# Two DMA queues put in a new order: plain loads and stores on SP, quarter loads alone on the ACT ring, twelve whole pairs transposed by VectorE

## The chip, the cores and the metric

One core of one Trainium2 chip. The metric is device time in microseconds (us) of a whole execution. For one core, the state of a run is told from the other runs of the same kernel on the same chip: a run over 1.5% above the fastest is called slow and is left out of the ratios.

## The reference

```python
y = np.matmul(x, weight)                       # x: (16, 512, 768) f32, weight: (768, 768)
y = y.reshape(16, 512, 12, 64)                 # 12 heads of 64
y1, y2 = y[..., :32], y[..., 32:]
out1 = y1 * cos1 - y2 * sin1                   # rotary embedding: cos, sin of (512, 64),
out2 = y2 * cos2 + y1 * sin2                   # the same for every batch and head
out = np.concatenate([out1, out2], axis=-1).reshape(16, 512, 768)
```

A product of 8192 x 768 by 768 x 768 in half precision, and two multiplications and an addition per element after it.

## The kernel before

The 64 row tiles (128 rows by 768) are worked in 32 *pairs*. For a pair (n; halves s = 0, 1): SP loads the two tiles; ScalarE casts them to fp16 (`xc`); the tile is transposed to `xT`; TensorE does 24 matmuls into PSUM (`psy`); VectorE multiplies by cos and sin at once (`tq`, 3.36 us a pair); GpSimd adds (`ov`, 3.46 us a pair); the pair is stored with one DMA.

There are two ways to get `xT`. The plain way is six TensorE transposes into PSUM and a copy by ScalarE (0.80 us). The other leaves TensorE out: the tile is loaded in four *quarters*, each 32 partitions with rows of 768 bytes, so that VectorE's transpose in blocks of 32 x 32 (0.57 us) gives the whole transposition. Before, ten tiles go this way.

```python
    AHEAD = 7
    AHEAD_B = 6
    ALONE = 4
    def by_blocks(n, s):                       # ten tiles: second halves of pairs 9, 11, ... 27
        return s == 1 and n % 2 == 1 and 8 < n < NP - ALONE
    ...
    xpool = ctx.enter_context(tc.tile_pool(name="xpool", bufs=10))
    bpool = ctx.enter_context(tc.tile_pool(name="bpool", bufs=3))
    ...
    def load_blocks(n):
        ...
        for q in (0, 2, 1, 3):                 # half of the quarters on each queue
            eng = nc.sync if q % 2 == 0 else nc.scalar
            eng.dma_start(out=dst[ts(q, R)], in_=src[r, q])
    ...
    def upto(what, k):                         # casts and transposes run ahead of the matmuls,
        k += min(6, max(0, k - 31) // 4)       # and further ahead as the kernel goes on
        while done[what] < min(k, 2 * NP):
            n, s = divmod(done[what], 2)
            done[what] += 1
            if what == "cast":
                cast(n, s, nc.scalar)
            elif not by_blocks(n, s):
                transpose(n, s, nc.scalar)     # six on TensorE, then ScalarE's copy xT
    ...
    for n in range(2, NP):
        load_plain(n + AHEAD - 2)              # SP
        if n + 1 < NP and by_blocks(n + 1, 1):
            transpose_blocks(n + 1, 1)         # VectorE
        for s in (0, 1):
            for c in CHUNKS:
                mm(n, s, *c)
            upto("turn", 2 * n + s + 3)
            upto("cast", 2 * n + s + 5)
            ...                                # the last four pairs, half by half
        load_blocks(n + AHEAD_B)               # SP and ACT
        if n < NP - ALONE:
            if n >= 3:
                store(n - 3, nc.scalar)        # ACT
            rope_pair(n, ...)                  # VectorE and GpSimd
```

The order of instructions on each engine is that of the program: each engine's work, and the issues of SP and of ScalarE, run so without an exception. A transfer is issued by the engine that it is written on (SP, or ScalarE for the ACT ring), and no work that stands behind an issue of ScalarE began before that issue was over, the soonest 0.04 us after it. So an issue that has to wait holds up all that stands behind it (the trace below has ScalarE stand so until 86.29 us).

## Time and profile before

163.46 us, median of three runs (162.96 to 163.48). The profiled run (163.1 us, granted clock 0.991):

| | before |
|---|---|
| TensorE busy | 150.3 us of a span of 161.3 (93%) |
| one pair in the middle (from one multiply of VectorE to the next) | 4.57 and 4.23 us in turn |
| six transposes on TensorE | 0.33 to 0.35 us |
| half-idle DMA engines | about 121 to 137 us |
| longest stop of ScalarE for a transfer of the other queue whose data it did not need | 2.6 us |

The difference between 4.57 and 4.23 us is one tile's transposes. The lines themselves are in the prediction below.

### The profile page before, as it was taken

To read this page: it belongs to the slowest core of one execution; us is meant where nothing else is said; L and a number is where in the kernel's file an instruction comes from. 1 tells how busy PE (TensorE), PEld (TensorE's weight loads), DVE (VectorE), ACT (ScalarE), POOL (GpSimd) and SP (SyncE) were. 2 spreads that over 40 slices of the span, in tenths; PEclk is the share of its full clock that TensorE was granted. 3 is DMA by queue.
4 is the path that set the end of the run, shared out by engine and by line. 5 is a ranking of instruction groups with operands and counts; after the bars stand their busy time and mean duration, and the time that the engine had idled before them with its cause. 6 is when DMAs were issued, how large, how long until landed. Compare 5 with 4: busy or idle time off the path is not lost.

```text
span 161.3 us, 2793 instructions
## 1 busy us (share of the span) xinstructions
PE 150.3 (93%) x1110; PEld 95.1 (59%) x1110; DVE 120.6 (75%) x70; ACT 91.6 (57%) x115; POOL 110.4 (68%) x41
## 2 busy tenths in 40 slices
PE   7789899999999999999998999999999999999920
PEld 2345566666566666666665666656666666665610
DVE  0555967876668788987878488885878697699980
ACT  3340867666677485656584977488767887200000
POOL 0000297778776787878878757788678776999990
PEclk9999999999999999999999999999999999999996
DMA  4999999999999999999999999999996555399655
GB/s 142 356 406 399 401 403 357 289 344 403 306 403 370 355 387 286 397 353 359 334 318 318 407 328 411 378 349 409 391 406 266 195 195 196 150 393 380 247 200 195
DMA packets 23757, 53.17 MB, mean 330 GB/s; under 512 B 2368, under 2 KB 7872, under 8 KB 23744
## 3 DMA queue, kind: packets, MB, share of 16 engines
q1 hardware_dynamic: 11952, 26.09, 46.5%
q10 hardware_dynamic: 11792, 26.91, 44.1%
q8 instruction: 8, 0.13, 0.3%
q14 instruction: 5, 0.04, 0.1%
HBM read 27.82 MB, written 25.17 MB: 328 GB/s over the span
## 4 chain that ended last, share of the span: by engine, by line
PE 61%; DMA 24%; ACT 5%; SPq 2%; POOL 2%; DVE 1%; issue 1%; ACTq 1%; POOLq 0%; DVEq 0%
PE psy L169 51%; DMA xs<-in_x_dram 17%; PE pt L126 8%; DMA w_raw<-in_weight_dram 4%; DMA xb<-in_x_dram 3%; ACT xc L76 3%; PE psz L169 2%; ACT xT L76 2%; POOL ov L194 2%; DVE tq L183 1%; SPq L83 1%; ACTq L243 1%; SPq L102 1%; POOLq L364 0%; POOLq L194 0%
## 5 line engine op out<-in xcount | busy, mean ns | idle before, releaser
L194 POOL TENSOR_TENSOR ov<-tq 128x1536 f32<-128x1536 f32 (+2 forms) x37 | 110.2, 2988 | 46.8 <-DVE tq L183 46.8
L169 PE MATMUL psy<-w_sb,xT 128*128 128x512 f16 (+1 forms) x732 | 127.5, 326 | 1.0 <-ACT xT L76 0.9
L183 DVE TENSOR_TENSOR tq<-psy,csn 128x3072 f32<-128x3072 f32 (+3 forms) x39 | 103.0, 2658 | 27.9 <-PE psy L169 26.2
L169 PEld LDWEIGHTS <-xT 128*128 128x128 f16 x768 | 73.1, 98 | 45.2 <-ACT xT L76 1.2
L76 ACT COPY xT<-pt 128x768 f16<-128x768 f16 x52 | 41.3, 800 | 38.0 <-PE pt L126 29.1
L76 ACT CAST xc<-xs 128x768 f16<-128x768 f32 x52 | 45.9, 903 | 8.8 <-DMA xs<-in_x_dram 8.7
L126 PEld LDWEIGHTS <-xc 128*128 128x128 f16 x324 | 22.1, 98 | 10.2 <-ACT xc L76 1.9
L126 PE MATMUL pt<-ident,xc 128*128 128x128 f16 x324 | 26.4, 219 | 1.8 <-ACT xT L76 0.7
L76 ACT CAST xc<-xb 128x768 f16<-128x768 f32 x10 | 9.1, 908 | 0.0
L247 PE MATMUL cold_ps<-cold 128*128 128x512 f16 x16 | 5.9, 516 | 1.2 <-DVE cold L252 1.2
L169 PE MATMUL psz<-w_sb,xT 128*128 128x512 f16 (+1 forms) x36 | 6.3, 326 | 0.0
L133 DVE STREAM_TRANSPOSE xT<-xc 128x384 f32<-128x384 f32 x10 | 5.7, 568 | 0.0
L110 DVE CAST w_sb<-w_raw 128x768 f16<-128x768 f32 x6 | 3.4, 560 | 2.1 <-DMA w_raw<-in_weight_dram 2.1
L78 DVE CAST xc<-xs 128x768 f16<-128x768 f32 x2 | 1.9, 946 | 3.6 <-DMA xs<-in_x_dram 3.6
L183 DVE TENSOR_TENSOR tq<-psz,csn 128x512 f32<-128x512 f32 (+1 forms) x5 | 4.3, 897 | 0.1
L247 PEld LDWEIGHTS <-cold 128*128 128x128 f16 x16 | 1.8, 127 | 3.4 <-issue 2.2
L78 DVE COPY xT<-pt 128x768 f16<-128x768 f16 x2 | 1.1, 558 | 1.7 <-PE pt L126 1.7
L76 ACT ACT_TABLE_LOAD x1 | 1.3, 1283 | 1.1 <-PEq L350 1.1
L252 DVE MEMSET cold<- 128x256 uint32 x1 | 0.3, 272 | 0.9 <-PEq L350 0.9
L148 PE MATMUL psy<-cold 128*128 128x512 f16 x2 | 0.8, 379 | 0.0
L226 DVE TENSOR_TENSOR ov<-psz,tq 128x512 f32<-128x512 f32 x1 | 0.7, 691 | 0.0
L222 DVE TENSOR_TENSOR psz<-psz,csn 128x512 f32<-128x512 f32 x1 | 0.7, 690 | 0.0
(8 smaller groups left out, 1.7 us busy)
## 6 DMA issues: line engine op xcount, KB each, us to landing
out_dram<-ov ACTq DMA_DIRECT2D x28, 768.0 KB, 6.5
xs<-in_x_dram SPq DMA_DIRECT2D x54, 384.0 KB, 6.9
out_dram<-ov ACTq DMA_DIRECT2D x7, 384.0 KB, 2.3
w_raw<-in_weight_dram SPq DMA_DIRECT2D x6, 384.0 KB, 7.7
xb<-in_x_dram SPq DMA_DIRECT2D x20, 96.0 KB, 5.6
xb<-in_x_dram ACTq DMA_DIRECT2D x20, 96.0 KB, 4.7
out_dram<-ov SPq DMA_DIRECT2D x1, 256.0 KB, 2.8
csn<-in_cos_dram SPq DMA_DIRECT2D x1, 128.0 KB, 7.8
```

Source lines behind the costliest of these rows:

```text
L76: eng.copy(out=o, in_=i_)
L78: eng.tensor_copy(out=o, in_=i_)
L83: nc.sync.dma_start(out=xss[n, s], in_=x[b].rearrange("(p r) h -> r p h", r=SB)[r])
L102: eng.dma_start(out=dst[ts(q, R)], in_=src[r, q])
L110: nc.vector.tensor_copy(out=w_sb[:, t, e], in_=w_raw[:, t, e])
L126: nc.tensor.transpose(pt[:, t, e, :], xc[:, t, e, :], ident)
L133: nc.vector.transpose(out=xT.bitcast(FP32).rearrange("p t m e -> p (t m e)"), in_=x16.pop((n, s)).bitcast(FP32),)
L169: nc.tensor.matmul(ps, xTT[n, s][:, t, e, :], w_sb[:, t, e, lo:hi], start=((t, e) == CHUNKS[0] and not joined), stop=((t, e) == CHUNKS[-1] ...
L183: nc.vector.tensor_tensor(out=tqs[n][:, :, c0:c1].rearrange("p j (h d) -> p j h d", d=D), in0=ps.rearrange("p (h d) -> p h d", d=D) .unsqu ...
L194: eng.tensor_tensor(out=ovs[n][:, ds(c0, w)].rearrange("p (h t d) -> p h t d", t=2, d=HD), in0=tq[:, 0].rearrange("p (h t d) -> p h t d", ...
L243: eng.dma_start(out=dst, in_=src)
L247: nc.tensor.matmul(cold_ps, cold[:, 0:P], cold, start=True, stop=True)
```

## The change

Twelve whole pairs (7, 9, ... 29) go by VectorE's blocks, so 24 tiles instead of ten. SP carries all plain loads and, except in the tail, all stores, in one program order. ScalarE, which used to issue the stores, now issues only the quarter loads before the tail: two at a time, each holding one quarter of both halves of the pair (192 KB), three and two iterations before the iteration that casts the pair. The intent: fewer transposes on TensorE, no ScalarE standing before a store, and no plain load stuck behind small pieces (in the trace of before, 3 KB packets of SP's queue took up to 2.25 us, 0.12 us in the median).

```diff
-    AHEAD_B = 6
     ALONE = 4
+    BLOCKS = range(7, NP - 2, 2)
 ...
-    xpool = ctx.enter_context(tc.tile_pool(name="xpool", bufs=10))
+    xpool = ctx.enter_context(tc.tile_pool(name="xpool", bufs=8))
 ...
+    def load_quarters(n, quarters):
+        b, r = where(n, 0)
+        if quarters[0] == 0:
+            xss[n] = bpool.tile([P, 2, H], FP32, tag="xb", name="xb")
+            xss[n, 0], xss[n, 1] = xss[n][:, 0], xss[n][:, 1]
+        src = ...
+        for q in quarters:
+            nc.scalar.dma_start(out=dst[ts(q, R)], in_=src[r, q])
 ...
+    def goal(k):
+        return k + min(6, max(0, k - 31) // 4)
 ...
             if what == "cast":
                 cast(n, s, nc.scalar)
-            elif not by_blocks(n, s):
+            elif n in BLOCKS:
+                transpose_blocks(n, s)
+            else:
                 transpose(n, s, nc.scalar)
+    def cast_in(m):                            # the iteration that casts pair m
+        return next(n for n in range(NP) if goal(2 * n + 6) > 2 * m)
 ...
-        load_blocks(n + AHEAD_B)
+        for m in BLOCKS:
+            for lead, quarters in ((3, (0, 2)), (2, (1, 3))):
+                if n == cast_in(m) - lead:
+                    load_quarters(m, quarters)
         if n < NP - ALONE:
-            if n >= 3:
-                store(n - 3, nc.scalar)
+            store(n - 2, nc.sync)
```

More of the change, by code (lines that the diff above doesn't have):

```diff
@@ L41 @@
     AHEAD = 7
-    AHEAD_B = 6
     ALONE = 4
+    BLOCKS = range(7, NP - 2, 2)
     def where(n, s):
         return 2 * (n // SB) + s, n % SB
-    def by_blocks(n, s):
-        return s == 1 and n % 2 == 1 and 8 < n < NP - ALONE
     konst = ctx.enter_context(tc.tile_pool(name="konst", bufs=1))
@@ L85, in load, with load_pair @@
         )
-    def load_plain(n):
+    def load_pair(n):
         for s in (0, 1):
-            if n < NP and not by_blocks(n, s):
+            if n < NP and n not in BLOCKS:
                 load(n, s)
-    def load_blocks(n):
-        if n >= NP or not by_blocks(n, 1):
-            return
-        b, r = where(n, 1)
-        xss[n, 1] = bpool.tile([P, H], FP32, tag="xb", name="xb")
-        src = x[b].rearrange("(j a r) (q k) -> r q a j k", r=SB, a=R, q=NQ)
-        dst = xss[n, 1].rearrange("p (j k) -> p j k", j=NQ)
-        for q in (0, 2, 1, 3):
-            eng = nc.sync if q % 2 == 0 else nc.scalar
-            eng.dma_start(out=dst[ts(q, R)], in_=src[r, q])
+    def load_quarters(n, quarters):
[3 more added lines that the diff above has]
+            xss[n, 0], xss[n, 1] = xss[n][:, 0], xss[n][:, 1]
+        src = x[b : b + 2].rearrange("b (j a r) (q k) -> r q a (b j) k", r=SB, a=R, q=NQ)
+        dst = xss[n].rearrange("p s (j k) -> p (s j) k", j=NQ)
+        for q in quarters:
+            nc.scalar.dma_start(out=dst[ts(q, R)], in_=src[r, q])
     wv = weight.rearrange("(p t e) n -> t e p n", t=NT, e=2)
@@ L115, in cast @@
         src = xss.pop((n, s))
-        if by_blocks(n, s):
+        if n in BLOCKS:
             src = src.rearrange("p (j a t e) -> p t (j a) e", j=NQ, t=NT, e=2)
@@ L254 @@
     for n in (0, 1):
-        load_plain(n)
+        load_pair(n)
     for t, e in CHUNKS:
@@ L260 @@
     for n in range(2, AHEAD):
-        load_plain(n)
+        load_pair(n)
     done = {"cast": 4, "turn": 4}
+    def goal(k):
+        return k + min(6, max(0, k - 31) // 4)
     def upto(what, k):
-        k += min(6, max(0, k - 31) // 4)
+        k = goal(k)
         while done[what] < min(k, 2 * NP):
@@ L311 @@
     for n in range(2, NP):
-        load_plain(n + AHEAD - 2)
-        if n + 1 < NP and by_blocks(n + 1, 1):
-            transpose_blocks(n + 1, 1)
+        load_pair(n + AHEAD - 2)
         for s in (0, 1):
@@ L324 @@
                     store(n, nc.scalar, s * H, (s + 1) * H)
-        load_blocks(n + AHEAD_B)
+        for m in BLOCKS:
+            for lead, quarters in ((3, (0, 2)), (2, (1, 3))):
+                if n == cast_in(m) - lead:
+                    load_quarters(m, quarters)
         if n < NP - ALONE:
-            if n >= 3:
-                store(n - 3, nc.scalar)
+            store(n - 2, nc.sync)
             rope_pair(n, H if n == NP - ALONE - 1 else 2 * H)
         if n == NP - ALONE - 1:
-            for m in (n - 2, n - 1, n):
-                store(m, nc.scalar)
+            for m in (n - 1, n):
+                store(m, nc.sync)
     rope_last(NP - 1, 1)
```

## The prediction

> **What bounds the kernel now.** I read the busy line and the 40 slices first, then the chain that ended last, the waits, and the timeline of the middle, last the windows for the DMA rate.
>
> The page, busy line and slices:
>
> ```profile
> PE 150.3 (93%) x1110; PEld 95.1 (59%) x1110; DVE 120.6 (75%) x70; ACT 91.6 (57%) x115; POOL 110.4 (68%) x41
> ...
> PE   7789899999999999999998999999999999999920
> ...
> DMA  4999999999999999999999999999996555399655
> GB/s 142 356 406 399 401 403 357 289 344 403 306 403 370 355 387 286 397 353 359 334 318 318 407 328 411 378 349 409 391 406 266 195 195 196 150 393 380 247 200 195
> ```
>
> TensorE is full from slice 4 to the tail. The DMA engines are full too, but only to slice 30 (about 121 us): then all of x is loaded, and some 16 us run at half load. So TensorE binds, and DMA is a close second with a reserve at the end.
>
> The waits, whole run (engine, whom it waited for, total, times, longest):
>
> ```profile
> ACT xT L76 <- PE pt L126: 29.1, 37, 1.9
> DVE tq L183 <- PE psy L169: 26.2, 28, 2.1
> ...
> ACT xT L76 <- DMA xb<-in_x_dram: 2.6, 1, 2.6
> ACT xT L76 <- DMA xs<-in_x_dram: 2.2, 1, 2.2
> ...
> PE psy L169 <- ACT xT L76: 0.9, 2, 0.7
> ```
>
> ScalarE and VectorE wait for TensorE, hardly the other way round. The chain of work, in order of time (start, us, what), around one of the rare stalls:
>
> ```profile
> 73.84 1.95 PE psy L169 x12
> 75.79 0.35 PE pt L126 x6
> ...
> 78.58 7.95 DMA xs<-in_x_dram
> 86.53 0.02 issue
> 86.55 0.02 ACTq L243
> 86.56 0.04 issue
> 86.60 0.41 ACTq L243
> 87.01 0.04 issue
> 87.05 0.81 ACT xT L76
> 87.91 2.12 PE psy L169 x12
> ```
>
> Two readings. First, the price list of TensorE: the 12 matmuls of a row tile cost 1.95 us, its six transposes 0.33 to 0.35 us. Second, the stall: ScalarE, which issues the stores, stood before a store until a *load* landed at 86.53, though no data ties them. The trace's records show all transfers rotating over eight completion semaphores in program order, so a transfer waits for the landing of the eighth before it, on whichever queue. That held up ScalarE's copy xT, and TensorE behind it.
>
> Check of the bound: from 16.87 to the last matmul at 154.15 are 137.3 us. 61 tiles x 1.95 = 119.0, plus 50 transposed tiles x 0.335 = 16.8, makes 135.7. So 1.6 us are stalls, all else is TensorE work.
>
> [...] the windows show 401 GB/s at 8 to 24 us, before any quarter load, and much less while quarters fly:
>
> ```profile
> 8.00:24.00 16.00, 15.04 (x111) 9.20 (x111) 11.02 (x12) 8.38 (x11) 4.67 (x2) 1.00 1.03 401
> 28.00:30.00 2.00, 2.00 (x18) 1.35 (x17) 1.43 (x1) 1.30 (x3) 2.00 (x1) 1.00 1.03 263
> 40.90:43.40 2.50, 2.33 (x19) 1.39 (x18) 1.29 (x2) 1.57 (x3) 2.25 (x1) 1.00 1.10 273
> 61.40:62.60 1.20, 1.20 (x14) 0.84 (x12) 1.20 (x1) 0.00 (x0) 1.20 (x1) 1.00 0.72 113
> ```
>
> (last columns: DMA share and GB/s). [...] both queues together never pass 411 GB/s in a slice.
>
> **The change, part by part.**
>
> *TensorE.* Before, ten tiles (second halves of odd pairs 9 to 27) are transposed by VectorE; after, both halves of pairs 7, 9, ... 29, that is 24. Fourteen tiles lose six transposes: 14 x 0.335 = 4.7 us off the engine that binds. The tail (pairs 28 to 31 alone, some 20 us from the end of pair 27's matmuls) keeps its work, so this passes to the end undiminished if nothing else binds.
>
> *ScalarE.* 14 copies xT x 0.80 = 11 us go. Of its issues the 36 stores fall to 8 and the 20 quarters grow to 48, about 0.4 us each: +8 us. It was idle enough; about even. What counts is that it no longer stands before a store: the waits of 2.2 and 2.6 us shown above should go, and with them perhaps 1 us of the 1.6 us of stalls.
>
> *VectorE.* 14 more block transposes at 568 ns: +8.0 us, to 128.6. In the middle a block pair needs 3.36 + 2 x 0.57 = 4.50 us of VectorE against 3.90 us of TensorE; the plain pair after it 3.36 against 3.90 + 0.67 = 4.57. Over two pairs: 7.86 against 8.47 us, 93% full, so it still fits. One joint is tight: early on, when little lead has built up, the first half's transpose comes right after the multiply of the pair before, ending 0.1 + 3.36 + 0.57 = about 4.0 to 4.1 us after that pair's last matmul, and TensorE wants it after 3.90. I estimate 0.2 us for each of pairs 7 to 17: about 1.2 us. (Before, a whole tile time more was left.)
>
> *DMA.* Bytes stay, 53.2 MB: at 403 GB/s, 132 us. Per block tile, 3 KB rows become four 768 B pieces. The 24 slices from 24 to 121 us have a mean of 361 GB/s, so 97 x (1 - 361/403) = 10 us were lost over ten block tiles, about 1 us each. Part of this is the stretch at 61 us (113 GB/s), where the records show plain-load packets stuck up to 2.2 us behind quarters on the same queue; quarters alone on the ACT queue should end that. I put the loss at 0.5 us for each of 24 tiles: 12 us. The sum 132 + 2 (start) + 12 = 146 us, plus 2 to 3 us around 22 us where SP has loaded its seven pairs and must wait for the first store before it goes on, fits into 157 us but uses up most of the reserve. Per two pairs DMA needs 3.15 MB / 403 = 7.8 us plus 2 x 0.5 = 8.8 us against TensorE's 8.47: slightly too slow through the middle, paid from the lead of loads over matmuls, and caught up after pair 29 is loaded.
>
> *One order on SP.* A load of pair n+6 comes after the store of pair n-2, which is ready when GpSimd's add ends, about 0.1 + 3.36 + 0.1 + 3.46 = 7.0 us after that pair's matmuls. The load then has three pairs (some 13 us) until its cast early on, against a median of 6.9 us to landing. The quarters 1 and 3 have only about 6.6 us, and each is twice as large as before (192 KB, where 96 KB took 4.7 to 5.6 us). I estimate another 1 us of stalls in all from late quarters and late loads.
>
> Sum: -4.7 - 1.0 + 1.2 + 1.0 = -3.5; 163.46 - 3.5 = 160.0. The order is evidently matched (two quarters and a store in each pair, two plain loads in every second: eight transfers in two pairs, so each waits for its like of two pairs ago), which makes me lean a little lower: **159.7 us**.
>
> **The rivals.** *DMA becomes the bound.* For it: DMA is full to 121 us, and 24 tiles in small pieces at the old loss of 1 us make 24 us: 132 + 2 + 3 + 24 = 161, no room left; that gives 162 to 166. Against it: the worst stretches belong to SP's mixed queue, and all loads are in at 121 us, eight pairs before they are needed. *VectorE becomes the bound in the middle*, its in-order transposes waiting for casts and delaying the multiply that frees PSUM: 161 to 163. Against it: casts run two tiles ahead, and the waits show VectorE idle 26.2 us for TensorE. *All goes well*: the saved transposes and most old stalls: 163.46 - 4.7 - 1.3 = 157.5.
>
> **Range and chances.** Best case 157.5, a mild DMA shortage 162.5: the range is 157.2 to 162.8. The line for 2% is 160.2, just above my centre, so faster 0.55, within 2% 0.40, slower (over 166.7, only if DMA binds outright) 0.05.
>
> **What would show each step.** Right: transposes x240 instead of x324 in TensorE's group, stream transposes x24 at 568 ns, the two-pair period near 8.5 us (before 8.8) in the middle, TensorE's busy time near 145 us, no wait of ScalarE's copies for a store's semaphore, the half-idle DMA stretch at 125 to 140 us gone or short. Wrong: ScalarE's casts waiting for xb several times by over 1 us and TensorE for xT behind them (quarters late); TensorE waiting for VectorE's xT by more than 0.3 us a pair (the tight joint is worse); slices staying under 350 GB/s with no idle stretch after (DMA binds); or plain loads landing late because SP stands before stores.

The sum stands at -4.7 - 1.0 + 1.2 + 1.0 = -3.5, so 160.0 us, and 159.7 with the lean.

## The result, and the profile after

The changed kernel took 174.16 us, median of four runs (173.54 to 176.84), against 163.47 us of before in the same rounds. The ratio is 1.0657 (95% interval 1.0613 to 1.07): slower by 6.6%. A ratio here is the mean time of one kernel's fast runs over that of the other's in the same rounds, so it is not quite the ratio of the medians.

The profiled run after is the longest of the four (176.84 us, state slow), but the state is not what makes it slow: the three fast runs, of 173.54 to 174.44 us, have mean clocks of 0.953 to 0.962, hardly better than its 0.953. The low clock is part of the effect, as the windows below show. From the page, in this order the busy line, the slices of TensorE and its granted clock, and the two groups of transposes (busy us and mean ns after the first bar, idle time before them after the second):

```profile
PE 151.3 (86%) x1026; PEld 92.1 (53%) x1026; DVE 127.2 (73%) x84; ACT 81.4 (46%) x101; POOL 110.3 (63%) x41
...
PE   7889999999989999996089999899339999999940
...
PEclk9999999999999999999957999999966999999996
...
L124 PE MATMUL pt<-ident,xc 128*128 128x128 f16 x240 | 20.5, 223 | 8.0 <-ACT xc L73 7.3
...
L131 DVE STREAM_TRANSPOSE xT<-xc 128x384 f32<-128x384 f32 x24 | 13.0, 561 | 6.5 <-ACT xc L73 6.4
```

The work is as planned: 240 transposes on TensorE instead of 324, 24 on VectorE. But there are two holes in TensorE's row, in slice 19 and in slices 28 and 29 (counted from 0), and the clock is low just after each. In the middle the kernel otherwise runs better than before. Times of a pair, from the start of VectorE's multiply of the pair before it to that of its own, read from the traces:

| pair | 9 to 15, each | 16 | 19 | 23 | start of pair 26 |
|---|---|---|---|---|---|
| before | 4.23 / 4.57 | 4.57 | 4.57 | 4.23 | 133.92 us |
| after | 4.23 | 13.74 | 6.35 | 12.16 | 147.71 us |

So nearly all the loss lies in three pairs (of the others only pair 8 is much longer than before, 5.42 us against 4.57). Counted over 4.23 us, the three cost 9.51 + 2.12 + 7.93 = 19.6 us; against their own times before, 18.9 us. The kernel is 13.8 us late at pair 26, so the other pairs have *gained* 5.1 us.

The waits after (total, times, longest), and the first of SP's queue:

```profile
ACT xT L73 <- issue: 17.3, 2, 9.7
...
PE psy L167 <- ACT xT L73: 7.5, 3, 6.6
```

```profile
SPq L241 <- POOL ov L192: 93.4, 28, 13.3
```

ScalarE stands idle before its copy xT twice, for 17.3 us together, and TensorE waits for it. "issue" means that nothing which the copy itself needs was missing: ScalarE was busy with, or standing before, something else in its order. SP, meanwhile, spends its time standing before stores until GpSimd's add is done. The timeline around the first hole (start, us, what, and in brackets the idle time before it) shows what ScalarE stood before:

```profile
79.74 4.61 SPq L241 DMA_DIRECT2D out_dram<-ov  x2
...
81.01 0.50 PE L124 MATMUL pt<-ident,xc 128*128 128x128 f16 x6
...
86.29 0.94 ACTq L100 DMA_DIRECT2D xb<-in_x_dram  x2
87.27 0.80 ACT L73 COPY xT<-pt 128x768 f16<-128x768 f16 x1 [9.69 <-issue]
...
88.13 6.79 PE L167 MATMUL psy<-w_sb,xT 128*128 128x512 f16 x24 [6.62 <-ACT xT L73]
```

The transposes of 81.01 were done by 81.5, and their copy could have begun then. It began at 87.27, because ScalarE issued two quarter loads at 86.29 first. Those loads need no data that the kernel computes, and their buffer was free: the first two quarters of the same pair had gone into it at 74.70 and 75.14. The issue and landing times of single transfers in the records, with the semaphore that each raises when it lands, tell why they were late:

```
semaphore 99   store of pair 11 (SP)              issued 71.26   landed 78.51
semaphore 99   store of pair 13 (SP)              issued 79.74   landed 86.27
semaphore 99   first of the late quarter loads    issued 86.29
               of pair 19 (ACT ring)
```

All transfers of the kernel share eight semaphores, numbered 99, 101, 103, 104, 105, 107, 108 and 109. The built program gives them out in turn, in the order in which it lists the transfers. Each transfer waits for the landing of the one that had its semaphore before, on whichever queue that was: of the 134 transfers in this trace 126 have such a forerunner, and all of them went out after it had landed, the soonest 0.02 us after. Here the quarter load, which stands *ahead* of pair 13's store in the source by one iteration, was given that store's semaphore after it. It could not be issued before a store that was itself waiting for GpSimd.

The smaller loss, in pair 19, has the same cause: a quarter load went out at 106.18, 0.02 us after the store of pair 16 (SP) had landed on its semaphore, and ScalarE's copy behind it came after 5.78 us of idle. Here VectorE lost the time: its block transposes, which stand before the multiply of pair 19 in its order, waited 1.00 and 0.92 us for ScalarE's casts. Pairs 20 and 21 then took only 3.72 and 3.85 us.

The second hole is the same as the first, on the chain that ended last (start, us, what):

```profile
117.07 7.66 DMA out_dram<-ov
...
124.75 0.34 ACTq L100
...
129.71 0.82 PE pt L124 x6
130.53 3.84 PE psy L167 x12
```

A store lands at 124.73, and only then does ScalarE's next load (L100 is the quarter load) go out. The last two lines show the after-effect: 12 matmuls took 3.84 us and six transposes 0.82, against 1.95 and 0.35 in the kernel before. The windows after the first hole (columns: window, busy us and counts of PE, PEld, DVE, ACT and POOL, then granted clock, DMA share, GB/s) show why:

```profile
84.00:86.00 2.00, 0.00 (x0) 0.00 (x0) 0.64 (x1) 0.00 (x0) 1.28 (x1) 1.00 0.86 341
86.00:88.00 2.00, 0.00 (x0) 0.00 (x0) 0.00 (x0) 0.73 (x2) 2.00 (x1) 0.71 0.99 249
...
90.00:92.00 2.00, 2.00 (x9) 0.97 (x7) 0.24 (x1) 1.87 (x3) 0.00 (x0) 0.50 1.10 225
92.00:94.00 2.00, 2.00 (x9) 1.05 (x8) 0.00 (x0) 0.00 (x0) 0.00 (x0) 0.58 1.06 383
94.00:96.00 2.00, 2.00 (x18) 1.26 (x16) 0.98 (x1) 0.71 (x2) 0.00 (x0) 1.00 0.31 114
```

The clock fell to half (0.50 from 90 to 92 us) some 5.3 us into the idle time, at 86.8 by the mean of that window, and came back at 93.7 by that of its own, 5.5 us after the work had resumed. So 24 matmuls took 6.79 us where they take 3.90. This closes the sum of pair 16: 6.62 us of waiting and 2.89 us of slow matmuls are 9.51 us, and 13.74 less 4.23 is 9.51.

### The profile page after: what moved, and what is told of

It is laid out like the page before. It is cut to its first block, busy times and chain, and to the rows that moved or that the text cites. A ratio compares the mean times of both kernels' runs of the same rounds, so it can differ in the third digit from the quotient of the medians.

```text
span 175.0 us, 2632 instructions
## 1 busy us (share of the span) xinstructions
PE 151.3 (86%) x1026; PEld 92.1 (53%) x1026; DVE 127.2 (73%) x84; ACT 81.4 (46%) x101; POOL 110.3 (63%) x41
## 4 chain that ended last, share of the span: by engine, by line
POOL 33%; PE 30%; issue 15%; DMA 12%; DVE 3%; ACTq 2%; SPq 1%; ACT 1%; POOLq 1%; DVEq 0%
POOL ov L192 33%; PE psy L167 24%; DMA out_dram<-ov 4%; DMA xs<-in_x_dram 4%; DMA w_raw<-in_weight_dram 4%; PE pt L124 3%; DVE tq L181 3%; ACTq L100 2%; PE psz L167 2%; SPq L80 1%; ACT xc L73 1%; POOLq L371 0%; POOLq L192 0%; DVEq L181 0%; ACT xT L73 0%
## 5 line engine op out<-in xcount | busy, mean ns | idle before, releaser
L167 PE MATMUL psy<-w_sb,xT 128*128 128x512 f16 (+1 forms) x732 | 130.3, 334 | 7.6 <-ACT xT L73 7.5
L167 PEld LDWEIGHTS <-xT 128*128 128x128 f16 x768 | 75.0, 100 | 56.5 <-ACT xT L73 8.2
L73 ACT COPY xT<-pt 128x768 f16<-128x768 f16 x38 | 30.3, 800 | 52.9 <-PE pt L124 28.2
L73 ACT CAST xc<-xs 128x768 f16<-128x768 f32 x38 | 33.2, 904 | 15.4 <-DMA xs<-in_x_dram 10.7
L124 PE MATMUL pt<-ident,xc 128*128 128x128 f16 x240 | 20.5, 223 | 8.0 <-ACT xc L73 7.3
L124 PEld LDWEIGHTS <-xc 128*128 128x128 f16 x240 | 16.7, 100 | 15.7 <-ACT xc L73 9.9
L73 ACT CAST xc<-xb 128x768 f16<-128x768 f32 x24 | 21.4, 902 | 2.6 <-DMA xb<-in_x_dram 2.6
L131 DVE STREAM_TRANSPOSE xT<-xc 128x384 f32<-128x384 f32 x24 | 13.0, 561 | 6.5 <-ACT xc L73 6.4
```

Source lines behind the costliest of these rows:

```text
L73: eng.copy(out=o, in_=i_)
L124: nc.tensor.transpose(pt[:, t, e, :], xc[:, t, e, :], ident)
L131: nc.vector.transpose(out=xT.bitcast(FP32).rearrange("p t m e -> p (t m e)"), in_=x16.pop((n, s)).bitcast(FP32),)
L167: nc.tensor.matmul(ps, xTT[n, s][:, t, e, :], w_sb[:, t, e, lo:hi], start=((t, e) == CHUNKS[0] and not joined), stop=((t, e) == CHUNKS[-1] ...
```

## The experiments

The theory to test: *ScalarE is stopped by shared completion semaphores; the new order of transfers pairs its quarter loads with transfers of SP that stand behind a store.* The rivals: *B*, the DMA engines cannot carry 24 tiles in 768-byte pieces; *C*, VectorE has become the bound; *D*, plain loads come too late because SP stands before stores. All runs were correct. e1 to e4 share one chip and one set of runs of before, e5 to e8 another set, e9 to e11 a third.

| run | median us | ratio to before [95%] | longest pair of 9 to 25, us |
|---|---|---|---|
| after | 174.16 | 1.0657 [1.0613, 1.07] | 13.74 |
| e1 no growing lead | 168.38 | 1.0321 [1.0263, 1.0379] | 4.47 |
| e2 quarters on SP | 163.34 | 1.0015 [0.9955, 1.0075] | 7.47 |
| e3 seven block pairs | 170.93 | 1.0477 [1.0435, 1.0518] | 12.45 |
| e4 eight block pairs | 170.57 | 1.0462 [1.0419, 1.0504] | 12.95 |
| e5 quarters on SP, loads nine pairs ahead | 159.1 | 0.9633 [0.9558, 0.9708] | 5.23 |
| e6 stores on ACT | 160.97 | 0.98 [0.9735, 0.9864] | 5.62 |
| e7 stores on ACT, loads nine ahead | 164.94 | 1.0034 [0.9965, 1.0104] | 5.35 |
| e8 loads nine ahead alone | 178.76 | 1.0882 [1.0802, 1.0962] | 13.33 |
| e9 seven 4-byte loads, spread | 179.43 | 1.089 [1.0798, 1.0982] | 8.22 |
| e10 seven 4-byte loads, early | 173.01 | none (one fast run, 168.9 us) | 4.24 |
| e11 e5 with eleven pairs ahead | 161.18 | 0.9795 [0.97, 0.989] | 7.36 |

### e1: without the growing lead

In the changed kernel two sets of quarter loads fall together where the lead of the casts grows (iterations 13, 16 and 21). Without the growth there is one set in every iteration, and two quarter loads and a store in each pair with two plain loads in every second pair make exactly eight transfers per two pairs.

```diff
     def goal(k):
-        return k + min(6, max(0, k - 31) // 4)
+        return k
```

> The changed kernel with the growing lead of casts and transposes taken out (the lead stays at its starting value), so a second set of quarter loads never falls into the same pair as the first; built, no quarter load after pair 11 waits for a store any more. Theory A (ScalarE stands before a quarter load until a store lands that itself needs TensorE to go on): no stop of ScalarE over 4 us after 60 us, TensorE's waits for ScalarE's xT under 3 us in all, two pairs in about 8.5 us through the middle, the whole at 159 to 166 us (the tail may pay for the missing lead). Theory B (24 block tiles in 768 B pieces make DMA the bound): 172 us or more, since bytes and pieces stay. Theory C (VectorE's 24 transposes bind): 172 or more too, with VectorE full in the middle.

The stops in the middle are gone: pairs 9 to 25 take 4.23 us (one 4.47), with all 24 block tiles, all pieces and all bytes. This refutes B and C for the middle. But the expectation missed in three points: the total is 168.38 us, not 159 to 166; TensorE waits 6.7 us for ScalarE's xT, not under 3; and one stop of ScalarE remains, in pair 26 (7.79 us):

```profile
127.51 0.80 ACT L73 COPY xT<-pt 128x768 f16<-128x768 f16 x1 [7.76 <-DMA xs<-in_x_dram]
```

It is a stop of the same kind: a quarter load of pair 29 went out at 127.15, after a plain load of SP on the same semaphore had landed at 127.12. Even so pair 26 starts at 132.54 us, earlier than before (133.92). The 3% are lost after it: from there to the end e1 takes 33.3 us and before 27.4. That this is the missing lead fits, but no run shows it alone.

### e2: the quarter loads on SP

```diff
         for q in quarters:
-            nc.scalar.dma_start(out=dst[ts(q, R)], in_=src[r, q])
+            nc.sync.dma_start(out=dst[ts(q, R)], in_=src[r, q])
```

> The changed kernel with the quarter loads issued by SP, in their place in the program order; ScalarE issues none, so nothing can stop it. Same bytes, same pieces, same 24 block tiles, same growing lead. Theory A: the two long stops go, 159 to 166 us; SP may be late with some quarters, which then shows as casts waiting for xb. Theory B: 172 us or more. Theory C: 172 or more.

Nothing is left in the middle for ScalarE to issue, so no semaphore can stop it, and the two stops are gone: 174.16 becomes 163.34 us, with the same work. What is left is late data (the slices of TensorE, and its line of the waits):

```profile
PE   7789899999999999999989999989693999999920
```

```profile
ACT xc L73 <- DMA xs<-in_x_dram: 23.6, 12, 5.3
```

SP now stands before stores with all loads behind it, and pairs 22, 23 and 25 take 5.41, 5.89 and 7.47 us. So rival D is real in this variant, though not what stopped the changed kernel; e5 and e8 take this up.

### e3 and e4: seven and eight block pairs

Where the order is matched up to pair 19, seven block pairs (7 to 19) should escape and eight should not.

```diff
-    BLOCKS = range(7, NP - 2, 2)
+    BLOCKS = range(7, 21, 2)        # e3
+    BLOCKS = range(7, 23, 2)        # e4
```

> The changed kernel with block pairs 7 to 19 only (14 tiles instead of 24). Built, no quarter load after pair 11 waits for a store. Theory A: no long stop; 14 tiles against ten of before save 1.3 us of TensorE: 160 to 164 us. Theory B (cost per block tile): before plus 4/14 of the loss of 10.7 us, some 166 us.

> As the run with pairs 7 to 19, with pair 21 by blocks as well (16 tiles). One difference in the built program: a quarter load of pair 19 now waits for the store of pair 13. Theory A: one long stop of ScalarE of 8 to 10 us near 80 us, TensorE waiting over 5 us for xT there, 6 to 11 us slower than the run with seven pairs. Theory B: 1 us slower than it. Theory C: under 1 us slower.

The expectation for e3 missed: it has a stop too, and e4 is no slower than it. The timelines of e3 and e4:

```profile
75.49 9.69 ACTq L100 DMA_DIRECT2D xb<-in_x_dram  x2
85.28 0.87 ACT L73 CAST xc<-xs 128x768 f16<-128x768 f32 x1 [9.95 <-DMA xs<-in_x_dram]
```

```profile
89.19 0.80 ACT L73 COPY xT<-pt 128x768 f16<-128x768 f16 x1 [9.89 <-issue]
```

In e3 the second of two quarter loads waited until a plain *load* landed at 84.84. SP had issued it only at 77.68, behind a store that could not go out before 76.14. I had looked in the built order only for quarter loads that wait for stores. The mechanism is the same, but it is wider than I had put it: here a plain load of SP did it, because it had itself stood behind a store. e3 and e4 cut the work of the blocks by a third and more and stop for as long, which speaks against B once more.

### e5, e8: plain loads nine pairs ahead, with and without e2

```diff
-    AHEAD = 7
+    AHEAD = 9
 ...
-    xpool = ctx.enter_context(tc.tile_pool(name="xpool", bufs=8))
+    xpool = ctx.enter_context(tc.tile_pool(name="xpool", bufs=12))
```

e5 is e2 with this edit, e8 the changed kernel with it.

> The kernel with the quarter loads on SP, with the plain loads issued two pairs earlier (lead of nine instead of seven pairs, twelve plain buffers instead of eight). If the stops of that kernel at pairs 22 to 25 (5.4, 5.9 and 7.5 us a pair instead of 4.2) come from plain loads that stand too late in SP's order behind stores, they go: 157.5 to 160.5 us, pair 26 reached at 128 to 130 us of the span. If they come from a shortage of DMA bandwidth, nothing moves: about 163 us.

> The changed kernel with the plain loads two pairs earlier and twelve plain buffers, stores on SP and quarter loads on ScalarE as in the changed kernel. Theory A: quarter loads still wait for transfers that SP holds behind stores, so at least one stop of ScalarE over 6 us stays: 167 us or more. Theory D (all of the loss is plain loads that come too late): 157 to 162 us.

They part as the theory has it. In e8 the stops stay (pair 16 13.33 us, pair 23 11.74), so late loads did not cause them. The timeline of e8 at the first (the second is 7.16 us long):

```profile
89.39 0.80 ACT L73 COPY xT<-pt 128x768 f16<-128x768 f16 x1 [9.29 <-issue]
```

In e5, where the quarters no longer stop ScalarE, the same edit is worth 4% (1.0015 to 0.9633, each against the runs of before in its own rounds), and the kernel is faster than before and than e2: 159.1 us. Its page:

```profile
PE 145.5 (93%) x1026; PEld 90.0 (58%) x1026; DVE 126.7 (81%) x84; ACT 81.8 (52%) x101; POOL 110.4 (71%) x41
...
PE   6899999999999999999998999999998999999920
...
DMA  4999999999999999999999999999999999568555
```

TensorE's busy time is 145.5 us, VectorE at 81% and the DMA engines at full use do not hold it up, and pair 26 starts at 128.91 us, 5.0 us earlier than before.

### e6, e7: the stores back on the ACT ring

The other way to take the two sides apart: ScalarE issues quarters *and* stores, SP has only loads, so that no transfer of SP stands behind a store.

```diff
         if n < NP - ALONE:
-            store(n - 2, nc.sync)
+            store(n - 2, nc.scalar)
 ...
-                store(m, nc.sync)
+                store(m, nc.scalar)
```

e6 is this alone, e7 has the edit of e5 as well.

> The changed kernel with one part undone: the stores are issued by ScalarE as before (after the same pair's quarter loads), SP has loads alone. Same 24 block tiles and pieces. Theory A in its narrower form (what stops ScalarE are transfers that SP issues behind a store): loads on SP no longer stand behind stores, so the two stops of 9 us go: 158 to 163 us. Theory B or C (pieces, VectorE): 172 us or more.

> The kernel with the stores back on ScalarE, with the plain loads two pairs earlier and twelve plain buffers. Theory A: 157.5 to 161.5 us, no slower than the run without the earlier loads by more than 1 us.

e6 is faster than before by 2.0%, clear of noise, though whether it passes the 2% line is unclear (interval 0.9735 to 0.9864). It has no pair over 5.62 us between 9 and 25; ScalarE's copy waits for a store four times, 3.9 us at most, where one stop had lasted 9.7. So it is not the quarter loads on the ACT ring as such that cost the time. e7 missed. Its timeline shows a new stop, much earlier:

```profile
36.07 0.80 ACT L73 COPY xT<-pt 128x768 f16<-128x768 f16 x1 [6.09 <-DMA out_dram<-ov]
```

ScalarE waited for a store to land, and pair 5 takes 10.43 us. The records show a shared semaphore once more, now within ScalarE's own queue: its store of pair 1 went out at 35.61, after the store of pair 0 had landed at 35.54 on the same semaphore; in e6 the two have different ones. I read this as the early rotation moved by the two more pairs of loads at the start; no run takes that alone.

### e9, e10: seven loads of four bytes

This takes the disputed cause by itself. To e1, whose middle is clean, seven loads of four bytes on SP are added. Nothing reads them. Spread over every second iteration they make nine transfers per two pairs: by the built program, 16 of the 24 quarter loads of pairs 11 to 21 then wait for a transfer of SP. Put all in iteration 2, the same seven leave the middle at eight transfers, and none of the 24 waits so; in e1 two do, the first ones. (The text on record counts from pair 9 and says 17, and none of those in e1; by the built program it is 18, of which the two of pair 9 wait in e1 too.)

```diff
+    TINY = {8: 1, 10: 1, 12: 1, 14: 1, 16: 1, 18: 1, 20: 1}     # e9
+    TINY = {2: 7}                                                # e10
+    spare = konst.tile([P, 64], FP32)
+    def tiny():                      # k: a new column each time
+        nc.sync.dma_start(out=spare[0:1, k : k + 1], in_=sin[0:1, k : k + 1])
 ...
                     load_quarters(m, quarters)
+        for _ in range(TINY.get(n, 0)):
+            tiny()
```

> Take the variant without the growing lead (e1_noramp, 4.23 us per pair up to pair 25, 1.0321 of before) and add seven loads of four bytes each on SP, one in every second pair of iterations 8 to 20. They carry nothing and no engine reads them; nine transfers instead of eight per two pairs make the rotation of the eight completion semaphores slip: 17 of the quarter loads from pair 9 to pair 21 then wait, by the built program, for a store or load of SP (in e1_noramp none of those do). Shared semaphores (my theory): quarter loads of pairs 17 to 21 wait for stores issued in the same iteration, ScalarE's xT comes late, and several pairs between 9 and 21 take 5 us or more instead of 4.23; the run is at least 3% longer than e1_noramp, so 1.06 of before or more. Rival (the stops come from bandwidth, late data or the amount of work): 28 bytes cost nothing, every pair stays at 4.23 and the ratio stays 1.03.

> Control of the run before: the same seven loads of four bytes, all in iteration 2, so that the rotation is eight per two pairs again from pair 9 on (by the built program none of the quarter loads of pairs 11 to 21 waits for a transfer of SP). Shared semaphores: 4.23 us per pair in the middle and within 1% of e1_noramp, 1.02 to 1.045 of before, and at least 2% shorter than the run before. Rival that the extra transfers themselves cost the time (seven more issues on SP): both runs lengthen alike.

The windows from 65 to 125 us of e9, of e10 and of e1, in this order (columns as above):

```profile
65.00:125.00 60.00, 53.35 (x361) 32.44 (x359) 46.15 (x25) 28.93 (x36) 41.89 (x13) 0.97 1.01 316
```

```profile
65.00:125.00 60.00, 60.00 (x426) 37.80 (x425) 53.86 (x29) 33.85 (x42) 49.22 (x15) 1.00 1.04 366
```

```profile
65.00:125.00 60.00, 59.92 (x427) 37.59 (x425) 53.46 (x29) 32.27 (x40) 48.96 (x15) 1.00 1.05 371
```

Twenty-eight bytes, spread, took 6.6 us of TensorE's work out of these 60 us: pair 12 took 8.22, pair 18 5.85 and pair 20 6.85 us, and from pair 11 to pair 25 e9 needed 68.65 us, e10 59.29, e1 59.53. In pair 12 of e9 ScalarE again stood before a quarter load:

```profile
69.27 0.80 ACT L82 COPY xT<-pt 128x768 f16<-128x768 f16 x1 [5.51 <-DMA xs<-in_x_dram]
```

The same bytes placed early cost nothing there. So the position of transfers in the rotation alone makes these stops, with data, pieces and bytes the same. The fast runs agree: e9 has 177.66 and 177.97 us, e10's one fast run in the same rounds 168.9.

One part of the control missed. As a whole e10 took 173.01 us in the median, 2.7% more than e1 and not within 1%; only its one fast run, 168.9 us, is as short. Its first pairs are disturbed by the early shift (pair 7 8.24 us, against 5.17 in e1) and pair 26 takes 9.20 us, with a stop of 7.5 us like that of e1. e9 has such an early disturbance too (pair 7 9.67 us): by the built program a quarter load of pair 9 waits there for the store of pair 4, in e1 for that of pair 3. The profiled runs of e9 and e10 are both slow; the comparison rests on the pair times of the middle, where the mean clock of e10 was 1.00, and e9 has 177.66 us for its shortest run.

### e11: eleven pairs ahead

```diff
-    AHEAD = 9        # e5, and bufs=12
+    AHEAD = 11       # and bufs=14
```

> The best version (quarters on SP, plain loads nine pairs ahead, 0.963 of before) with eleven pairs ahead and two more plain buffers. If late loads are what is left in its pairs of 5.2 us (16 and 25), these shrink to 4.23 and it gains up to 1%: 0.95 to 0.965. If the deeper queue only lets more loads stand ahead of the quarters of the same pair on SP, nothing is gained or it loses 1 to 2%: 0.965 to 0.985.

The second case holds, inside its range of 0.965 to 0.985: 0.9795 of before (two fast runs; unclear at the 2% line), no better than e5's 0.9633, though the two were measured in different rounds. In the profiled run (slow) pair 16 takes 4.78 us and pair 25 7.36, where e5 has 5.18 and 5.23. Nine pairs ahead is the version to keep. What is left in e5's two pairs of 5.2 us was not settled.

## Why the prediction was wrong

The prediction was 159.7 us, in 157.2 to 162.8; it gave "slower" a chance of 0.05.

- **TensorE, -4.7 us: right.** The transposes are 240, and e5 shows the busy time of 145.5 us that was expected ("near 145"). The changed kernel's own 151.3 us comes from matmuls at half clock (0.50 twice within the work, for 6.83 us each).
- **The two-pair period near 8.5 us: right** wherever nothing stops: twice 4.23.
- **VectorE's tight joint, +1.2 us, and DMA "slightly too slow through the middle": too pessimistic.** Pairs 9 to 15 of the changed kernel run at 4.23 us, and so do nearly all of e1, which moves 371 GB/s from 65 to 125 us with all the quarters in it. The rivals of the prediction, DMA or VectorE as the bound, did not come about.
- **Late quarters and late loads, +1.0 us: not what happened.** Late loads cost much in e2 only. In the changed kernel ScalarE's casts waited 10.7 us for plain loads in the whole run, in the kernel before 8.7 already, and e8 has the stops with the loads two pairs earlier.
- **A sum that was wrong, on a point that decided nothing.** Under ScalarE it counts +8 us for issues. But 28 stores fewer and 28 quarter loads more leave their number the same, so ScalarE was relieved by the copies' 11 us: its busy time fell from 91.6 to 81.4 us.
- **The step that failed** is under ScalarE and in the leaning at the end: "What counts is that it no longer stands before a store", counted as -1.0, and "The order is evidently matched (...) so each waits for its like of two pairs ago". The prediction had seen the eight semaphores in the trace of before, where they cost 2.6 us at most, and then counted the transfers of a regular pair. It also took the rotation to follow the program's order, and it does not quite: the first late quarter of pair 19 stands before the store of pair 13 in the source and after it in the rotation. Only for the quarter loads of pairs 13 to 17 and the first two of pair 19 is the order matched throughout. The growing lead of the casts puts two sets of quarters into one iteration at 13, 16 and 21, and from pair 19's late quarters on the rotation no longer always meets its like: by the built program 12 of the last 22 quarter loads come after a transfer of SP on their semaphore. ScalarE then stands before SP's transfers, which stand before GpSimd, whose input depends on TensorE, which needs ScalarE. In place of -1.0 there were +19.6 us in three pairs: 6.6 us of waiting and 2.9 of half clock in the first stop, 7.9 in the second, 2.1 in the one between them.
- **The sign that would have told it** was named: "no wait of ScalarE's copies for a store's semaphore" stood among the signs of right. But it was kept for the result, though the irregular iterations could be counted from `goal` and `cast_in` by hand; and no rival had it.

The step is shown from two sides. Taking either party off (e2: the quarters to SP; e6: the stores off SP) removes the long stops, and moving only the rotation brings stops into a clean kernel (e9) or does not (e10). That the growing lead is what unmatched it is shown by e1. The extra 2.1 us of pair 19 are put down to the same cause by the trace alone; no run removes them by themselves.

## What to carry to other kernels

A transfer can wait for one that has nothing to do with it, if they share a completion semaphore (here a quarter load went out 0.02 us after another pair's store had landed, and ScalarE's copy behind it came after 9.69 us of idle); so don't let an engine that computes issue loads whose rotation reaches into a queue that stands before stores, or count the whole order, its irregular iterations above all, before trusting it. A stop that leaves TensorE idle can cost more than itself: after 6.6 us of waiting, 24 matmuls took 2.9 us more at half clock. When a change adds no work and a few pairs take three times as long as the rest, look at the pair times first: averages of busy time say nothing of it.
